# Seven block products in every feed-forward stage, with the modulation products moved to TensorE

## The chip, the cores and the metric

The kernel runs on one core of a Trainium2 chip. The metric is the device time of one execution in microseconds (us), from the first to the last instruction with what lies around them. All inputs are float32.

## The reference

Two layers over 640 tokens of width 1024: 512 latent tokens and 128 context tokens. Each layer has a feed-forward network (FFN), a token mixer (attention in layer 0, a gated recurrence in layer 1) and a second FFN. Each of these three is normalised before and after, shifted, scaled and gated by vectors that come from a modulation map.

```python
FFN_HIDDEN = ((8 * D_MODEL // 3 + 127) // 128) * 128          # 2816
def ada_pre(x, mod, j, g):
    return rmsnorm(x, g) * (1 + scale) + shift
def ada_post(x, y, mod, j, g, res_w):
    return x + res_w * gate * rmsnorm(y, g)
def swiglu(h, w_in, w_out):
    a, b = jnp.split(h @ w_in, 2, axis=-1)
    return (jax.nn.silu(a) * b) @ w_out
mod_ctx_all = jnp.einsum('d,lde->le', jax.nn.silu(c_ctx), w_mod) + b_mod
mod_lat_all = jnp.einsum('bd,lde->lbe', jax.nn.silu(c), w_mod) + b_mod[:, None]
```

The modulation map `w_mod` is 2 x 1024 x 9216: 36 column blocks of 512 over both layers, each multiplied by two vectors (latent and context).

## The kernel before

Activations lie transposed, features on partitions and the 640 tokens along the free axis, in two groups of 320 (`NG`). Each matrix is kept as a high part and a low part, so one product of a 128 x 128 weight tile with 320 tokens is three matmuls: high by high, high by low, low by high (in `run_jobs`, L444 and L449).

There are six stages in a row: p0 (FFN of layer 0), p1 (attention), p2 (second FFN of layer 0), p3 (FFN of layer 1), p4 (recurrence), p5 (second FFN of layer 1). A stage is a list of jobs. A plain job is one weight unit of up to eight 128 x 128 tiles against one or both groups. An FFN stage has 22 pairs of input-projection units (a gate unit and a value unit, 8 tiles each) whose results become one row block of `G`, and, after each part of the pairs, eight output-projection units that add that part's share into `Y`. Before the change `THIRDS` cuts the pairs into 7, 7 and 8. The first four pairs form the head: group 0 of all four, then group 1, so that the previous stage's normalisation of group 1 (`chain_gen`, with `post_gen` and `pre_gen`) can run meanwhile. The last eight output units form the tail: group 0 first, then group 1; five of these units lie in `H`, which is free by then.

In p5 alone, pairs from `FAST_FIRST` = 7 on are done in another way (`seven`): the pair is taken as a 2 x 2 block matrix (gate and value by the two halves of the 1024 features) and the activations as 2 x 2 blocks (feature halves by token groups), and the product is made of seven block products instead of eight, Winograd's form of Strassen's scheme. A block product (`product`, L476) is 4 tiles x 3 = 12 matmuls, so a pair takes 84 matmuls where the plain way takes 96. It needs sums of activation blocks, made once per stage by `sums_gen` into `T23` (in the place of `X`, which is spilled to DRAM by `spill_x` and read back by `unspill_x`), `T4` and the second half of `H`, and sums of weight blocks, made per pair on VectorE in `Quarter.follow`.

Weights come from DRAM by one queue (SyncE) into four raw buffers (`wraw`), are split by ScalarE (high part, L358) and VectorE (low part, L360) into a ring `whl` of eight quarters, of which a whole unit takes two and a quarter unit one. `prepare` converts ahead as far as `reach` and the ring allow.

Modulation blocks that are not needed at the start are made in the background of p0, p2 and p3 (12, 12 and 8 blocks, `mod_gen`): two loads of 1 MB bring a block of 1024 x 512, VectorE multiplies its eight 128-row tiles by the two vectors and adds them up (L763, L765: 16 instructions of 128 x 512 a block), and four matmuls of 32 x 256 with a matrix of ones sum over partitions (L775). `step_bg` takes one step of the first background generator at fixed places in the jobs. A first part of the modulation, before p0, is made by matmuls on 32 columns of the array (L871).

The order on each engine is that of the built program: a recording layer may move an instruction ahead of others that its inputs don't wait for, so engine order isn't source order.

## Time and profile before

| | |
|---|---|
| median of 3 runs | 2843.31 us (2841.24 to 2843.76) |
| profiled execution | 2848.25 us, its span 2846.3 us |
| TensorE matmul (PE) busy | 2775.4 us, 98% |
| VectorE (DVE) busy | 1849.1 us, 65% |
| ScalarE (ACT) busy | 1062.7 us, 37% |
| DMA share, mean rate | 33%, 100 GB/s |

The span is from the first to the last instruction of the profiled execution; 1.95 us lie around it. Busy times are unions over the whole span, so they say nothing of a single stage: the rows below are cut by stage. PE counts each fp32 matmul of the modulation as two instructions, and each 128 x 320 matmul as one.

### The profile page before, as it was taken

Reading aid. Unit: us, or ns where it says so; the run is one execution under the profiler, and the core shown is the slowest. Engines: PE = TensorE matmul, PEld = TensorE weight load, DVE = VectorE, ACT = ScalarE, POOL = GpSimd, SP = SyncE. Lnnn points to the kernel's source line nnn. Section 1 sums busy time; section 2 is a strip of 40 time slices with the busy share of each in tenths; the row PEclk is TensorE's granted clock in tenths of the full one; section 3 lists DMA queues with packets and bytes.
Section 4 is the critical chain, followed back from the end, with each engine's and each line's share of the span. In section 5 each row is a group of like instructions: output and inputs, shape, how many; then the busy total and the mean of one; then the engine's idle time right before and its main releaser. Section 6 shows DMA issues by size and latency. Waiting matters only on the chain.

```text
span 2846.3 us, 46837 instructions
## 1 busy us (share of the span) xinstructions
PE 2775.4 (98%) x19098; PEld 2710.3 (95%) x19098; DVE 1849.1 (65%) x3845; ACT 1062.7 (37%) x2100; POOL 0.2 (0%) x4
## 2 busy tenths in 40 slices
PE   7999999899998999999999999999999999999998
PEld 5999999899998999999999999999999999999997
DVE  6756653887777756656763554387667678656674
ACT  4222123466674422223332212243333345344453
POOL 0000000000000000000000000000000000000000
PEclk8999999999998999999999999999999999999999
DMA  8644433121123344445233433321121123323241
GB/s 265 185 134 148 147 111 90 43 59 52 46 72 97 109 136 138 153 140 163 60 100 108 130 123 89 89 61 49 56 60 56 56 59 104 87 70 92 73 133 38
DMA packets 424691, 283.32 MB, mean 100 GB/s; under 512 B 8442, under 2 KB 385820, under 8 KB 424220
## 3 DMA queue, kind: packets, MB, share of 16 engines
q1 hardware_dynamic: 423968, 280.13, 32.8%
q8 instruction: 150, 2.46, 0.4%
q14 instruction: 65, 0.53, 0.1%
q10 hardware_dynamic: 508, 0.20, 0.0%
HBM read 272.96 MB, written 7.34 MB: 98 GB/s over the span
## 4 chain that ended last, share of the span: by engine, by line
PE 89%; DVE 5%; ACT 4%; DMA 1%; issue 1%; ACTq 0%; DVEq 0%
PE mmps L444 48%; PE mmps L449 24%; PE mmps L476 6%; PE aux L1567 2%; PE mmps L1406 1%; PE aux L1375 1%; DMA wraw<-in_ffn_w_out 1%; DVE whl L360 1%; PE aux L514 1%; ACT p L1305 1%; PE aux L775 1%; PE aux L526 1%; PE aux L1376 1%; PE aux L1604 1%; ACT sq L1638 0%
## 5 line engine op out<-in xcount | busy, mean ns | idle before, releaser
L444 PE MATMUL mmps<-H,whl 128*128 128x320 f32 x6272 | 1256.3, 313 | 8.4 <-ACT H L603 6.6
L444 PEld LDWEIGHTS mmps<-H,whl 128*128 128x128 f32 x6272 | 1003.9, 189 | 22.6 <-issue 9.1
L449 PE MATMUL mmps<-H,whl 128*128 128x320 f32 x3136 | 786.0, 312 | 0.7 <-DVE whl L360 0.7
L358 ACT ACTIVATE whl<-wraw 128x1024 fp32r<-128x1024 f32 (+2 forms) x384 | 361.4, 941 | 1104.4 <-issue 533.1
L360 DVE TENSOR_TENSOR whl<-wraw,whl 128x1024 fp32r<-128x1024 f32 (+2 forms) x384 | 413.4, 1077 | 348.2 <-ACT whl L358 343.9
L449 PEld LDWEIGHTS mmps<-H,whl 128*128 128x128 f32 x3136 | 544.2, 189 | 1.1 <-DVE whl L360 1.0
L444 PE MATMUL mmps<-G,whl 128*128 128x320 f32 x2368 | 471.2, 312 | 6.1 <-ACT G L971 1.7
L444 PEld LDWEIGHTS mmps<-G,whl 128*128 128x128 f32 x2368 | 378.7, 189 | 12.6 <-issue 3.3
L765 DVE SCALAR_TENSOR_TENSOR macc<-wmod,CV,macc 128x512 f32<-128x512 f32 x448 | 306.7, 748 | 0.0
L449 PE MATMUL mmps<-G,whl 128*128 128x320 f32 x1184 | 295.2, 311 | 0.0
L444 PE MATMUL mmps<-G,H 128*128 128x320 f32 x960 | 217.2, 313 | 0.1
L449 PEld LDWEIGHTS mmps<-G,whl 128*128 128x128 f32 x1184 | 204.9, 189 | 0.0
L444 PEld LDWEIGHTS mmps<-G,H 128*128 128x128 f32 x960 | 161.7, 189 | 0.4 <-ACT Y L1133 0.4
L1135 DVE TENSOR_TENSOR Y<-Y,mmps 128x320 f32<-128x320 f32 x144 | 67.2, 485 | 140.8 <-PE mmps L449 140.1
L449 PE MATMUL mmps<-G,H 128*128 128x320 f32 x480 | 149.9, 312 | 0.0
L969 DVE TENSOR_TENSOR gm<-sa,mmps 128x320 f32<-128x320 f32 x146 | 65.9, 484 | 123.3 <-PE mmps L449 122.6
L476 PE MATMUL mmps<-H,whl 128*128 128x320 f32 x720 | 113.0, 310 | 1.0 <-ACT gm L994 1.0
L476 PEld LDWEIGHTS mmps<-H,whl 128*128 128x128 f32 x720 | 107.4, 188 | 1.2 <-ACT gm L994 1.2
L444 PE MATMUL mmps<-H,G 128*128 128x320 f32 x448 | 104.6, 315 | 0.0
L548 DVE TENSOR_TENSOR acc<-acc,sq 128x320 f32<-128x320 f32 x168 | 80.6, 489 | 24.9 <-ACT sq L547 23.8
L449 PEld LDWEIGHTS mmps<-G,H 128*128 128x128 f32 x480 | 90.8, 189 | 0.0
L476 PE MATMUL mmps<-T,whl 128*128 128x320 f32 x540 | 86.6, 310 | 0.0
(259 smaller groups left out, 2923.7 us busy)
## 6 DMA issues: line engine op xcount, KB each, us to landing
wraw<-in_ffn_w_in SPq DMA_DIRECT2D x192, 512.0 KB, 4.0
wmod<-in_w_mod SPq DMA_DIRECT2D x66, 1024.0 KB, 6.1
wraw<-in_ffn_w_out SPq DMA_DIRECT2D x64, 448.0 KB, 3.8
wraw<-in_hgrn_w_in SPq DMA_DIRECT2D x40, 512.0 KB, 3.9
wraw<-in_ffn_w_out SPq DMA_DIRECT2D x32, 512.0 KB, 4.2
wraw<-in_attn_w_in SPq DMA_DIRECT2D x24, 512.0 KB, 3.9
wm<-in_w_mod SPq DMA_DIRECT2D x4, 1024.0 KB, 11.0
wraw<-in_attn_w_out SPq DMA_DIRECT2D x8, 512.0 KB, 4.0
```

The costliest lines, as they stand in the source:

```text
L358: nc.scalar.activation(out=u.w[0][:, 0:nk, :], in_=src, func=AF.Copy)
L360: self.los.append(lambda: nc.vector.tensor_tensor(out=u.w[1][:, 0:nk, :], in0=src, in1=u.w[0][:, 0:nk, :].bitcast(F32), op=ALU.subtract))
L444: nc.tensor.matmul(out=ps[g][:, 0:NG], lhsT=w[0][:, a, :], rhs=rhs[:, r, b, g * NG:(g + 1) * NG], start=(i == 0 and r == 0), stop=False,)
L449: nc.tensor.matmul(out=ps[g][:, 0:NG], lhsT=w[1][:, a, :], rhs=rhs[:, 0, b, g * NG:(g + 1) * NG], start=False, stop=(i == last),)
L476: nc.tensor.matmul(out=ps[:, 0:NG], lhsT=w[a][:, k, :], rhs=j.operand(r, k), start=(j.first and k == 0 and n == 0), stop=(k == 3 and n == ...
L514: self.nc.tensor.matmul(out=ps[:, c0 + n:c0 + n + 1], lhsT=acc[:, b0:b0 + 128], rhs=self.ones, start=True, stop=True,)
L526: self.nc.tensor.matmul(out=ps[:, c0 + b0 + p0:c0 + b0 + 128], lhsT=y[:, n:n + 1].to_broadcast([128, 128]), rhs=self.ident[:, p0:128], sta ...
L548: return lambda: nc.vector.tensor_tensor(out=acc, in0=acc, in1=sq, op=ALU.add)
L765: nc.vector.scalar_tensor_tensor(out=acc[s], in0=w, scalar=cv, in1=acc[s], op0=ALU.mult, op1=ALU.add)
L969: nc.vector.tensor_tensor(out=t, in0=st[g], in1=ps, op=ALU.mult)
L1135: nc.vector.tensor_tensor(out=y, in0=y, in1=ps, op=ALU.add)
L1567: nc.tensor.matmul(out=ps[:, c * 128:(c + 1) * 128], lhsT=km[:, c * 128:(c + 1) * 128], rhs=self.view(Q2, c * 128, dims), start=True, stop ...
```

## The change

All four FFN stages take pairs 4 to 21 by seven block products (`FAST`); only the four head pairs stay plain. The parts become 4, 5, 6 and 7 pairs, so each stage has four rounds of output units instead of three, with the same matmuls in total. X is spilled and the activation sums are made in each stage, right behind the head. Half of `T4` moves into row block 7 of `G`, which no part uses any more. The modulation blocks are multiplied on TensorE (`mod_rows`): eight matmuls of 32 x 512 a block, four at a time on different 32 columns, straight from the loaded weights; the matrix of ones goes. Away from products only three raw buffers are filled ahead and at most three whole units stand in the ring.

```diff
-THIRDS = (range(0, 7), range(7, 14), range(14, 22))
+PARTS = (range(0, 4), range(4, 9), range(9, 15), range(15, 22))
-GAP0 = 2
-GAP2 = 2
-GAP3 = 3
+GAP0 = 1
+GAP2 = 1
+GAP3 = 2
-FAST_FIRST = 7
+FAST = range(4, 22)
+PLAIN_RAWS = 3
...
     def place(self, u):
+        if u.quarters == 2 and sum(x.quarters == 2 for x in self.ring) >= HL_BUFS:
+            return False
...
-        if self.first[n] == self.n_conv - 1:
+        near = self.jobs[n:n + 6]
+        if not any(isinstance(j, Product) for j in near):
             self.flush_lo()
+            self.ensure_dma(self.raw_done + PLAIN_RAWS - 1)
+        elif self.first[n] == self.n_conv - 1:
+            self.flush_lo()
...
+    def mod_rows(self, ps, CS, ts, i, half, first, last):
+        for k in range(4 * half, 4 * half + 4):
+            g = k % 4
+            self.nc.tensor.matmul(
+                out=ps[g * 32:(g + 1) * 32, 0:512], lhsT=CS[:, k, 30 - 2 * i:62 - 2 * i], rhs=ts[half][:, g, :],
+                start=first and half == 0, stop=last and half == 1, skip_group_check=True,
+            )
...
         for i in range(n):
-            acc = [self.mod_p.tile([128, 512], F32, name="macc", tag=f"macc{s}") for s in range(2)]
-            for k in range(KT):
-                w = ts[k // 4][:, k % 4, :]
-                for s in range(2):
-                    for _ in range(gap):
-                        yield
...
-                if k % 4 == 3 and i + 1 < n:
-                    ts[k // 4] = self.mod_load(first + i + 1, k // 4)
-            yield
+            for _ in range(16 * gap):
+                yield
             ps = self.aux_tile()
...
+            for half in range(2):
+                self.mod_rows(ps, CS, ts, i, half, True, True)
+            if i + 1 < n:
+                ts = [self.mod_load(first + i + 1, h) for h in range(2)]
+            yield
...
-        self.T4 = self.fast.tile([128, 2, 4, NG], F32R, name="T4")
+        low = self.G[:, :, 7, :].rearrange("p r (k t) -> p r k t", k=2)
+        high = self.fast.tile([128, 2, 2, NG], F32R, name="T4")
+        self.T4 = [low[:, :, 0, :], low[:, :, 1, :], high[:, :, 0, :], high[:, :, 1, :]]
...
     def fast_hooks(self, jobs, last_plain):
+        last_plain.after.append(self.spill_x)
         last_plain.after.append(lambda: self.bg.insert(0, gen))
...
-        for part, third in enumerate(THIRDS):
+        for part, third in enumerate(PARTS):
             for jj, j in enumerate(third):
-                if fast and j >= FAST_FIRST:
+                if j in FAST:
                     jobs += seven(jj, j)
                     continue
...
-        if fast:
-            head[-1].after.append(self.spill_x)
+        self.fast_hooks(jobs, head[-1])
...
+        if mods:
+            jobs[-16].before.append(lambda: self.drain([self.modgen]))
```

On TensorE in p2, around one modulation block. A row is a line, an instruction, what it writes and reads, and how many follow each other. Before, among output jobs (`G` by `whl`):

```order
L449 MATMUL mmps<-G,whl 128x320 x2
L444 MATMUL mmps<-G,whl 128x320 x4
L449 MATMUL mmps<-G,whl 128x320 x2
L775 MATMUL aux<-macc,one 32x256 x4
L444 MATMUL mmps<-G,whl 128x320 x4
L449 MATMUL mmps<-G,whl 128x320 x2
```

And of the change, from one block to the next, in the stretch of block products of the second part (`T_10060` is `T23`, `T_10061` the new half of `T4`, and `G` its other half):

```order
L763 MATMUL aux<-wmod,CS 32x512 x8
L484 MATMUL mmps<-T_10060,whl 128x320 x12
L484 MATMUL mmps<-H,whl 128x320 x12
L484 MATMUL mmps<-T_10060,whl 128x320 x12
L484 MATMUL mmps<-H,whl 128x320 x12
L484 MATMUL mmps<-G,whl 128x320 x6
L484 MATMUL mmps<-T_10061,whl 128x320 x6
L484 MATMUL mmps<-H,whl 128x320 x24
L484 MATMUL mmps<-T_10060,whl 128x320 x12
L484 MATMUL mmps<-H,whl 128x320 x12
L763 MATMUL aux<-wmod,CS 32x512 x8
```

TensorE now reads the loaded block (`wmod`) itself, and 108 matmuls stand between two blocks. In the built program this distance is 108, with a few of 102 or 114, for 17 of the 32 blocks, 204 or more for the blocks of p3, and 60 and 63 once each in p0 and p2, between the second and the third block and the first and the second.

On SyncE's queue at the beginning of p2, where loads of weights (`wraw`) and of modulation blocks (`wmod`) are issued in order. Before:

```order
L708 DMA wmod<-in_w_mod 128x4x512
L322 DMA wraw<-in_ffn_w_in 128x8x128 x8
L708 DMA wmod<-in_w_mod 128x4x512
L322 DMA wraw<-in_ffn_w_in 128x8x128 x2
L708 DMA wmod<-in_w_mod 128x4x512
L322 DMA wraw<-in_ffn_w_out 128x7x128 x6
L708 DMA wmod<-in_w_mod 128x4x512
```

And of the change:

```order
L716 DMA wmod<-in_w_mod 128x4x512 x2
L322 DMA wraw<-in_ffn_w_in 128x8x128 x7
L888 DMA xs<-X 128x5120
L322 DMA wraw<-in_ffn_w_out 128x4x128 x4
L716 DMA wmod<-in_w_mod 128x4x512 x2
L322 DMA wraw<-in_ffn_w_out 128x4x128 x3
L716 DMA wmod<-in_w_mod 128x4x512 x2
L322 DMA wraw<-in_ffn_w_out 128x4x128
```

Both halves of a block are now issued together, behind the matmuls of the block before, which release the buffers; the spill of X stands between the head's loads, and four output units' loads stand ahead of the second block's.

On VectorE in p2, at the output units of the first part. Before, products and sums of the modulation (`macc`) between the low parts of weights:

```order
L360 TENSOR_TENSOR whl<-wraw,whl 128x896
L765 SCALAR_TENSOR_TENSOR macc<-wmod,CV,macc 128x512 x5
L360 TENSOR_TENSOR whl<-wraw,whl 128x896
L360 TENSOR_TENSOR whl<-wraw,whl 128x1024 x2
L763 TENSOR_SCALAR macc<-wmod,CV 128x512
L782 TENSOR_TENSOR ms<-ms,aux 128x256
```

And of the change, the end of the sums of activation blocks (L924 to L939, L916 the low parts of their splits):

```order
L916 TENSOR_TENSOR H<-nt,H 128x320
L362 TENSOR_TENSOR whl<-wraw,whl 128x512
L916 TENSOR_TENSOR T_10060<-nt,T_10060 128x320
L938 TENSOR_TENSOR nt<-H,nt 128x320
L916 TENSOR_TENSOR T_10060<-nt,T_10060 128x320
L362 TENSOR_TENSOR whl<-wraw,whl 128x512
L135 TENSOR_TENSOR s_10310<-wraw 128x512
L939 TENSOR_TENSOR nt<-nt,H 128x320
L137 TENSOR_TENSOR wraw<-wraw 128x512
L916 TENSOR_TENSOR T_10061<-nt,T_10061 128x320
L362 TENSOR_TENSOR whl<-wraw,whl 128x512 x4
```

The `macc` instructions are gone, and the sums end just ahead of the weight sums and splits of the first pairs that are done by block products.

## Rows read from the trace of the kernel before

**Rows 1.** The page: the span and the engines' busy times.
```profile
span 2846.3 us, 46837 instructions
PE 2775.4 (98%) x19098; PEld 2710.3 (95%) x19098; DVE 1849.1 (65%) x3845; ACT 1062.7 (37%) x2100; POOL 0.2 (0%) x4
```

**Rows 2.** Windows of p0 to p3 and p5: PE, PEld, DVE, ACT, POOL; clock, DMA.
```profile
36.20:529.50 493.30, 488.96 (x3336) 475.24 (x3337) 304.16 (x533) 139.92 (x235) 0.00 (x0) 0.99 0.45 135
529.50:917.80 388.30, 363.98 (x2481) 345.56 (x2479) 307.25 (x837) 239.66 (x578) 0.00 (x0) 0.97 0.22 64
917.80:1401.40 483.60, 482.98 (x3314) 474.73 (x3315) 308.58 (x558) 136.09 (x234) 0.00 (x0) 0.99 0.42 127
1401.40:1882.60 481.20, 478.65 (x3290) 472.28 (x3289) 259.62 (x487) 136.55 (x236) 0.00 (x0) 1.00 0.34 102
...
2373.50:2846.30 472.80, 456.73 (x3103) 452.19 (x3102) 295.60 (x585) 205.49 (x416) 0.00 (x0) 0.98 0.29 86
```

**Rows 3.** Windows in p5: plain output jobs, then 7.5 pairs by block products.
```profile
2616.00:2666.00 50.00, 50.00 (x342) 49.94 (x341) 22.26 (x38) 10.30 (x15) 0.00 (x0) 1.00 0.25 73
2666.00:2758.00 92.00, 92.00 (x630) 92.00 (x629) 71.78 (x128) 53.40 (x109) 0.00 (x0) 1.00 0.31 88
```

**Rows 4.** Timeline of TensorE around one modulation block in p2.
```profile
1064.36 0.46 PE L449 MATMUL mmps<-G,whl 128*128 128x320 f32 x2
1064.74 0.64 PE L775 MATMUL aux<-macc,one 128*32 128x256 f32 x8
1065.31 0.85 PE L444 MATMUL mmps<-G,whl 128*128 128x320 f32 x4
```

**Rows 5.** Timeline of TensorE, modulation matmuls of the start.
```profile
44.26 1.06 PE L871 MATMUL mmps<-wmod,CS 128*32 128x512 f32 x8
45.14 1.90 PE L871 MATMUL mmps<-Y,CS 128*32 128x512 f32 x16
```

**Rows 6.** Groups by line: the modulation on VectorE and TensorE; busy us, mean ns.
```profile
L765 DVE SCALAR_TENSOR_TENSOR macc<-wmod,CV,macc 128x512 f32<-128x512 f32 x448 | 306.7, 748 | 0.0
L763 DVE TENSOR_SCALAR macc<-wmod,CV 128x512 f32<-128x512 f32 x64 | 30.1, 483 | 61.1 <-PE aux L775 61.0
L775 PE MATMUL aux<-macc,one 128*32 128x256 f32 x256 | 20.5, 391 | 0.0
```

**Rows 7.** DMA issues: count, size of one, median us to landing.
```profile
wraw<-in_ffn_w_in SPq DMA_DIRECT2D x192, 512.0 KB, 4.0
wmod<-in_w_mod SPq DMA_DIRECT2D x66, 1024.0 KB, 6.1
wm<-in_w_mod SPq DMA_DIRECT2D x4, 1024.0 KB, 11.0
xs<-X SPq DMA_DIRECT2D x1, 2560.0 KB, 8.4
```

**Rows 8.** Timeline of VectorE in p5: part of the activation sums.
```profile
2475.88 0.49 DVE L925 TENSOR_TENSOR nt<-H 128x320 f32<-128x320 f32 x1
2476.28 0.49 DVE L930 TENSOR_TENSOR nt<-H 128x320 f32<-128x320 f32 x1
```

**Rows 9.** Timeline of TensorE in p0's head, around a wait.
```profile
60.58 0.46 PE L444 MATMUL mmps<-H,whl 128*128 128x320 f32 x2
63.12 0.51 PE L449 MATMUL mmps<-H,G 128*128 128x320 f32 x1 [2.08 <-DVE G L360]
63.42 0.73 PE L444 MATMUL mmps<-H,G 128*128 128x320 f32 x2
...
66.62 0.50 PE L444 MATMUL mmps<-H,G 128*128 128x320 f32 x2
66.96 0.31 PE L449 MATMUL mmps<-H,G 128*128 128x320 f32 x1
```

**Rows 10.** Waits among p5's block products, 2666 to 2758: total us, times, longest.
```profile
ACT whl L358 <- PE mmps L476: 28.0, 38, 1.3
DVE s L134 <- DMA wraw<-in_ffn_w_in: 5.8, 6, 1.3
```

More of the change, by code (lines that the diff above doesn't have):

```diff
@@ L274, in setup @@
         self.CV = c.tile([128, KT, 2], F32, name="CV")
-        self.one = c.tile([128, 64], F32, name="one")
         self.ones = c.tile([128, 1], F32, name="ones")
@@ L382, in prepare @@
                 self.raw_done += 1
-        if self.first[n] == self.n_conv - 1:
+        near = self.jobs[n:n + 6]
[3 more added lines that the diff above has]
+        elif self.first[n] == self.n_conv - 1:
             self.flush_lo()
     def more_dma(self):
-        self.flush_lo()
-        self.ensure_dma(self.raw_done + RAW_BUFS - 1)
+        near = self.jobs[self.cur:self.cur + 6]
+        if any(isinstance(j, Product) for j in near):
+            self.flush_lo()
+            self.ensure_dma(self.raw_done + RAW_BUFS - 1)
     def held(self, kt):
@@ L754, in mod_gen @@
         for i in range(n):
[L755 to L778 removed]
+            for _ in range(16 * gap):
+                yield
+            ps = self.aux_tile()
+            for half in range(2):
+                self.mod_rows(ps, CS, ts, i, half, True, True)
+            if i + 1 < n:
+                ts = [self.mod_load(first + i + 1, h) for h in range(2)]
+            yield
             if i == 0:
[L780 removed]
+                nc.scalar.activation(out=ms, in_=ps[:, 0:512], func=AF.Copy)
             else:
[L782 removed]
+                nc.vector.tensor_tensor(out=ms, in0=ms, in1=ps[:, 0:512], op=ALU.add)
             yield
         yield
[L785 removed]
+        self.mod_fin([(first, n)], ms, self.aux_tile(), False)
         for p in range(first // 2, (first + n) // 2):
@@ L797, in startup @@
         S = self.st_p
-        CS = S.tile([128, KT, 34], F32, name="CS")
+        CS = self.mod_p.tile([128, KT, 62], F32, name="CS", tag="CS")
         nc.sync.dma_start(out=self.ident, in_=A["k_ident"])
@@ L841, in startup @@
         )
-        nc.vector.tensor_copy(CS[:, :, 2:4], self.CV)
+        self.mod_vectors(CS)
         ps = self.aux_tile()
@@ L867, in startup @@
             for i in range(2):
-                ts = loads[2 * half + i]
-                for k in range(KT):
-                    g = k % 4
-                    nc.tensor.matmul(
-                        out=ps[g * 32:(g + 1) * 32, :], lhsT=CS[:, k, 2 - 2 * i:34 - 2 * i],
-                        rhs=ts[k // 4][:, k % 4, :], start=(i == 0 and k < 4), stop=(i == 1 and k >= 4),
-                        skip_group_check=True,
-                    )
+                for h in range(2):
+                    self.mod_rows(ps, CS, loads[2 * half + i], i, h, i == 0, i == 1)
             nc.scalar.activation(out=ms, in_=ps[:, 0:512], func=AF.Copy)
@@ L941, in sums_gen @@
             yield from put(b, self.T23[:, 0, 0, k, :], self.T23[:, 0, 1, k, :])
-            yield from put(d, self.T4[:, 0, k, :], self.T4[:, 1, k, :])
+            yield from put(d, self.T4[k][:, 0, :], self.T4[k][:, 1, :])
             yield
@@ L953, in fast_hooks, with ffn_jobs @@
         products[-1].after.append(self.unspill_x)
-    def ffn_jobs(self, l, s, mods, gap, close, fast=False):
+    def ffn_jobs(self, l, s, mods, gap, close):
         nc = self.nc
@@ L977, in y_done @@
         def y_done(f, part):
-            return lambda ps, g: self.y_part(f, ps, g, part == 0, part == 2)
+            return lambda ps, g: self.y_part(f, ps, g, part == 0, part == len(PARTS) - 1)
         def seven(jj, j):
```

38 lines of the change are left out of this document (9 added, 29 removed).

## The prediction

> **What bounds the kernel now.** I read the page first, then windows cut at the stages, then the timeline of TensorE inside them. On the page TensorE's matmuls are busy for 2775.4 of 2846.3 us and VectorE for 1849.1 [rows 1]. The cut by stages says the same of each FFN stage: in p0, p2 and p3 TensorE is busy for 488.96 of 493.30, 482.98 of 483.60 and 478.65 of 481.20 us, in p5 for 456.73 of 472.80, while VectorE is busy for 304.16, 308.58, 259.62 and 295.60 us of them [rows 2]. So within a stage TensorE's instruction stream is the path, and a matmul less is time less, as long as nobody makes TensorE wait.
>
> What one matmul is worth comes from stretches in which it never waits: 342 in 50.00 us of plain output jobs and 630 in 92.00 us of block products, both 146 ns each [rows 3]. A block product's matmul costs no more than a plain one, and its VectorE work (71.78 of 92.00 us) fits under it.
>
> **The change, part by part. The products.** In p0, p2 and p3 18 pairs a stage go from 96 to 84 matmuls, 3 x 18 x 12 = 648; in p5, where 15 were done so already, 3 more pairs, 36. Together 684 x 0.146 us = 99.9 us less. The cuts into four parts add none: the output units have the same tiles in total.
>
> **The modulation on TensorE.** 32 blocks. What goes: one block's eight instructions on ones begin at 1064.74, and the two 128 x 320 matmuls ahead of them began at 1064.36; the next follow at 1065.31 [rows 4]. The two take 0.29 us, to 1064.65, so a block held TensorE for 0.66 us, and 32 for 21.1. That is a little more than its busy time of 20.5 us [rows 6]. What comes: eight matmuls of 32 x 512 a block, 16 instructions in the trace. At the start 8 of them begin at 44.26 and the next 16 at 45.14, 0.88 us later [rows 5]; 16 therefore take 1.76 us. Rows 4 show what surrounds them in a stretch of 128-wide matmuls: 0.66 us where two rounds over 256 columns take half of 0.88, 0.44; so 0.22 us is spent on changing over. A block then costs 1.76 + 0.22 = 1.98 us, 32 cost 63.4, and the net addition is 63.4 - 21.1 = 42.3 us.
>
> The rows say that four such instructions run at once on different 32 columns: eight of L775's, each lasting 391 ns [rows 6], fit into the 0.66 us. The Trainium skill (TensorE: Matmul & The Clock Gate, Part 3: Packing small matmuls) gives less for packing, 3.07x measured for four row tiles and 2.38x for three column tiles. By that page's 3.07 in place of 4 a block would cost an estimated 1.76 x 4 / 3.07 + 0.22 = 2.51 us and the sum would be 17 us worse; the trace has the same instruction in the same form, so I go by the trace.
>
> VectorE loses 306.7 + 30.1 us of products [rows 6]. It isn't the path, so this gives nothing directly; it pays for the work of the block products.
>
> So far -99.9 + 42.3 = -57.6 us.
>
> **Waits for the modulation's loads.** Before, VectorE waited for a block; now TensorE, in order, and everything of TensorE is queued behind. A block's two loads of 1 MB go out only when the block before has released the buffers, and the weight loads behind them in SyncE's queue wait with them. One alone lands in 6.1 us, four at once in 11.0 [rows 7]. For 17 blocks 108 matmuls stand between, 108 x 0.146 = 15.8 us: more than either, so 0; the bound above is 2 us each, if weight loads are in the way in SyncE's queue. Twice only 60 or 63 matmuls stand there, 8.8 and 9.2 us; and in p2 the queue holds four output units' loads ahead, the last of which waits for a raw buffer, so for a conversion. Between nothing (6.1 us and a little) and 8 us (11.0 and a blocked queue of some 6 us) I take 3 us each, nearer to the row for four at once. A wait is followed by slow matmuls: after 2.08 us of waiting in p0, the 13 matmuls from 63.12 to 66.62 begin 0.27 us apart, the 1.2 GHz level [rows 9]; at 0.146 they would take 1.9 us instead of 3.5, so 1.6 us are lost. Twice 4.6 us makes +9.
>
> **The activation sums.** They stand in every stage now, between the head and the third product of pair 4, behind 192 output matmuls and 24 of two products: 216 x 0.146 = 31.5 us. VectorE has 56 instructions a stage, which begin 0.40 us apart [rows 8], 22.4 us. In the same time it splits eight output units of 512 columns and the first quarters, at 71.78 us for 7.5 pairs [rows 3], 9.6 a pair: some 14 us. That is 36 against 31.5, but sums whose inputs are ready stand ahead of the head's end. Late by 0 to 5 us a stage; I take 0.5, +2 in all. Spilling X lands in 8.4 us [rows 7] and begins during the head's first half, when X is final: hidden.
>
> **The rest.** Without `macc`, the head of p0 may lose its wait of 2.08 us and the slow stretch behind it [rows 9]: between 0 and -3.7, I take -2. Three whole units in the ring and three raw buffers ahead: a head job lasts 24 x 0.146 = 3.5 us and a load lands in 4.0 [rows 7], so three loads in flight cover it; in the attention and recurrence stages the bodies' order on TensorE stays as it was. I take 0, between -3 and +6. In block products four raw buffers stay; the loads share the channel with the modulation, but ScalarE waits there mostly for ring places that TensorE frees (28.0 us against 5.8 us of waiting for loads on VectorE [rows 10]), so weights are split well ahead: 0, above 4.
>
> **The sum.** -57.6 + 9 + 2 - 2 = -48.6 us. The sum was made against the profiled execution, 2848.25 us, of which 1.95 lie outside its span; that one ran 4.94 us above the median of the runs shown. The change takes the same number from either: 2843.3 - 48.6 = 2794.7 us, 2795 rounded.
>
> **Rivals.** *Waits of some size everywhere.* If the sums come late by 4 us in each of four stages and the 17 close blocks wait 1 us each, 33 us come on top of the sum: 2828, at about 2806 to 2837 in all. For it: VectorE's 36 us against 31.5. Against it: in p5 the block products themselves never made TensorE wait for VectorE.
>
> *Nothing waits.* If the loads arrive and p0's head wait goes with its slow stretch, the sum is -57.6 - 3.7: 2782, reaching down to 2775 with something gained in the plain stages. For it: 6.1 us a load against 8.8.
>
> *Slower, through the clock.* TensorE now stops for DMA. If each of the 29 waited-for blocks (32 less the first of each stage) cost 2.0 us or more in all, the 57.6 us would be gone; with a wait of 2 us and the slow stretch of 1.6 behind it that is 29 x 3.6 = 104 us, 2890 us in all. It takes loads that are late by 2 us at 15.8 us distance, that is 17.8 us for what the slowest row has at 11.0. The Trainium skill (TensorE: Matmul & The Clock Gate, section HAM oscillation) has it as a rule that a matmul kernel which waits for DMA in each tile falls back to the slow clock each time. By that rule the trace agrees on a single wait, in rows 9, and shows none that repeats.
>
> *It doesn't do what it says.* If VectorE or ScalarE bounded the products, 12 matmuls less would give nothing; VectorE at 71.78 / 92.00 = 78% and ScalarE at 53.40 / 92.00 = 58% in them [rows 3] speak against it; a 512-wide addition a block, at most the 748 ns of L765 [rows 6] in 17.8 us, makes it 82%. It lies within the last two cases below.
>
> **How the numbers follow.** Forecast (2782 to 2806): 0.63. Nothing waits, or better (below 2782): 0.13. Waits everywhere (2806 to 2837): 0.18. No change within 0.2% (5.7 us, about what a measurement can tell): 0.03. Slower: 0.03. The predicted time is 2795; the range from 2777 to 2817 leaves out a little below and half of the second rival above. Faster has 0.63 + 0.13 + 0.18 = 0.94.
>
> **What would show it.** Right: p0, p2 and p3 last about 460 to 470 us, p5 about 467; no group of block products waits; modulation blocks take 2 us each with TensorE waiting for `wmod` only at one block each in p0 and p2. Wrong: waits on `wmod` at many blocks and a granted clock below 1 in those stages; TensorE waiting for the sums' low parts at the third product of a stage; or an attention stage longer than its 388.3 us [rows 2].

## The result, and the profile after

The median of four runs is 2781.02 us (2780.47 to 2782.12), against 2843.53 (2841.24 to 2845.24) for the kernel before in the same session: ratio 0.9781, interval 0.9764 to 0.9798. The predicted time was 2795, the range 2777 to 2817. The time is inside the range, 14 us below the forecast, where I had put the rival that nothing waits.

The page of the kernel after, against [rows 1]:

```profile
span 2778.7 us, 47467 instructions
...
PE 2715.6 (98%) x18670; PEld 2613.1 (94%) x18670; DVE 1977.8 (71%) x4285; ACT 1307.3 (47%) x2693; POOL 0.2 (0%) x4
```

The profiled execution took 2780.47 us, its span 67.6 us less than before's. The medians differ by 62.5 us: the profiled run of the kernel before ran 4.7 us above its median, so some 5 us of what follows are the spread of these two runs. The windows of p0 to p5, cut at the same matmuls as in [rows 2] (columns: stretch, its length, busy time of PE, PEld, DVE, ACT, POOL, clock, DMA share, GB/s):

```profile
36.70:513.90 477.20, 471.48 (x3223) 445.06 (x3223) 326.98 (x642) 216.36 (x420) 0.00 (x0) 0.99 0.48 151
513.90:891.90 378.00, 362.38 (x2466) 344.39 (x2467) 298.10 (x814) 240.29 (x579) 0.00 (x0) 0.97 0.19 56
891.90:1360.90 469.00, 466.86 (x3202) 444.29 (x3200) 329.77 (x669) 215.28 (x421) 0.00 (x0) 1.00 0.46 144
1360.90:1825.30 464.40, 461.84 (x3143) 445.15 (x3143) 329.09 (x669) 213.06 (x420) 0.00 (x0) 1.00 0.40 123
1825.30:2313.60 488.30, 480.25 (x3467) 473.43 (x3468) 355.01 (x789) 192.57 (x384) 0.00 (x0) 1.00 0.20 58
2313.60:2778.70 465.10, 450.71 (x3068) 446.65 (x3066) 320.01 (x645) 218.39 (x451) 0.00 (x0) 0.99 0.29 88
```

p0, p2 and p3 are 16.1, 14.6 and 16.8 us shorter, p5 is 7.7 shorter. Of the lengths that the prediction gave as signs of being right, 460 to 470 us, p0 with 477.2 misses; its own terms give 493.3 - 31.5 + 12 x 1.32 = 477.6 for p0, so that sign was set wrong, not the sum. The line that I had not expected is the second: p1, the attention, whose body the change doesn't touch, is 10.3 us shorter than its 388.3. TensorE stays busy in nearly all of each FFN stage, and VectorE has more to do in p0 (326.98 us for 304.16) although the modulation's sums have left it.

Two windows in p5 answer to [rows 3]:

```profile
2558.00:2608.00 50.00, 50.00 (x342) 49.88 (x341) 25.82 (x44) 16.18 (x29) 0.00 (x0) 1.00 0.30 90
2608.00:2700.00 92.00, 92.00 (x629) 91.90 (x628) 67.19 (x120) 50.11 (x100) 0.00 (x0) 1.00 0.29 83
```

342 and 629 matmuls, as before 342 and 630: the price of one has not moved. The timeline of TensorE around a modulation block among block products of p0 answers to [rows 4, 5] (columns: start, length of the row, instruction):

```profile
137.56 1.92 PE L484 MATMUL mmps<-H,whl 128*128 128x320 f32 x12
139.41 1.92 PE L763 MATMUL aux<-wmod,CS 128*32 128x512 f32 x16
141.26 2.02 PE L484 MATMUL mmps<-H,whl 128*128 128x320 f32 x12
143.12 1.92 PE L484 MATMUL mmps<-T,whl 128*128 128x320 f32 x12
144.88 1.92 PE L484 MATMUL mmps<-H,whl 128*128 128x320 f32 x12
```

Twelve matmuls undisturbed take 1.76 us, from 143.12 to 144.88. From 137.56 to 143.12 stand 24 of them and one block: 5.56 - 2 x 1.76 = 2.04 us for a block. The groups of TensorE and the DMA issues answer to [rows 6, 7]:

```profile
L763 PE MATMUL aux<-wmod,CS 128*32 128x512 f32 x512 | 64.7, 599 | 0.0
```

```profile
wmod<-in_w_mod SPq DMA_DIRECT2D x66, 1024.0 KB, 7.1
...
xs<-X SPq DMA_DIRECT2D x4, 2560.0 KB, 12.8
```

TensorE was idle for 0.0 us ahead of its 512 modulation instructions: no wait for `wmod` at all. A load of a modulation block now lands in 7.1 us where it took 6.1, the spill of X in 12.8 for 8.4. The view of the tile `wmod` gives the ends too, and SyncE's queue shows the place in p2 with 63 matmuls between two blocks:

```profile
DMA to landing us min/median/max: 5.0/7.1/9.6
```

```profile
942.03 1.23 SPq L716 DMA_DIRECT2D wmod<-in_w_mod  x2
```

The second of these loads goes out at 942.9 and lands 7.0 us later, at 949.9; its block begins at 952.2, 2.3 us after that.

The end of the sums on VectorE in p5 and the first block products on TensorE, against [rows 8]:

```profile
2392.08 0.88 DVE L916 TENSOR_TENSOR T<-nt,T 128x320 fp32r<-128x320 f32 x2
```

```profile
2405.90 3.68 PE L484 MATMUL mmps<-H,whl 128*128 128x320 f32 x24
2409.42 1.92 PE L484 MATMUL mmps<-T,whl 128*128 128x320 f32 x12
```

The last two low parts end at 2392.96, 12.9 us ahead of the first product, and the third product, the first that needs a sum, begins 24 matmuls later without a pause. In p0's head the wait of [rows 9] has shrunk to 0.23 us, and the matmuls behind it begin 0.147 us apart:

```profile
62.80 0.42 PE L457 MATMUL mmps<-H,G 128*128 128x320 f32 x1 [0.23 <-DVE G L362]
63.05 0.46 PE L452 MATMUL mmps<-H,G 128*128 128x320 f32 x2
63.35 0.31 PE L457 MATMUL mmps<-H,G 128*128 128x320 f32 x1
```

The longest sum of waits among p5's block products, 2600 to 2692, is of the kind of [rows 10]: ScalarE waits 22.4 us in all for places in the ring.

**Where p1's 10.3 us came from.** p1's window ends at the first matmul of p2's head. Ahead of it, at the joint, group 0 of p1 is normalised while TensorE runs p1's output products of group 1. The inverse root of the norm is a chain of thirteen instructions of 0.16 us on VectorE, from `rs_v` to the third `rs_y`. In the kernel before, VectorE's timeline there reads (left out between these rows are further links of the chain and other work):

```profile
906.89 0.16 DVE L521 TENSOR_SCALAR rs_v<-aux 128x3 f32<-128x3 f32 x1 [0.99 <-PE aux L514]
906.96 0.74 DVE L765 SCALAR_TENSOR_TENSOR macc<-wmod,CV,macc 128x512 f32<-128x512 f32 x1
...
908.24 0.74 DVE L765 SCALAR_TENSOR_TENSOR macc<-wmod,CV,macc 128x512 f32<-128x512 f32 x1
...
911.25 1.22 DVE L360 TENSOR_TENSOR G<-wraw,G 128x1024 fp32r<-128x1024 f32 x1
...
914.77 0.15 DVE L509 SCALAR_TENSOR_TENSOR rs_y<-rs_a,rs_y 128x3 f32<-128x3 f32 x1
```

From 906.89 to 914.77 are 7.9 us: VectorE put two products of the modulation, two low parts of weights and additions to `acc` between the links, and stood idle for 1.22 us of them itself. TensorE ran out of output products, as the kernel before's waits of TensorE from 903 to 920 show (the first is for L514, which sums `acc` over the partitions, so for the additions as well as for the chain):

```profile
PE aux L514 <- DVE rs_y L509: 3.8, 1, 3.8
```

Waits of 0.6 us for `rs_y` and 1.2 for `H` follow it.

In the kernel after, the same chain is through in 3.5 us, with one low part of a weight in it, and the view of TensorE's waits has no row there:

```profile
881.27 0.16 DVE L529 TENSOR_SCALAR rs_v<-aux 128x3 f32<-128x3 f32 x1 [0.63 <-PE aux L522]
881.35 1.21 DVE L362 TENSOR_TENSOR whl<-wraw,whl 128x1024 fp32r<-128x1024 f32 x1
...
884.78 0.16 DVE L517 SCALAR_TENSOR_TENSOR rs_y<-rs_a,rs_y 128x3 f32<-128x3 f32 x1
```

This could come from the modulation's products having left VectorE, or from the new order of weights.

The other end of p1's window has changed too, at the joint of p0 with p1. The kernel before waits 22.6 us behind p1's first matmul, inside p1's window (529.5 to 917.8):

```profile
552.18 1.44 PE L514 MATMUL aux<-ones,acc 128*128 128x1 f32 x6 [3.33 <-DVE acc L548]
```

The kernel after doesn't have this wait; it waits at the end of p0's window instead:

```profile
511.14 0.80 PE L522 MATMUL aux<-ones,acc 128*128 128x1 f32 x6 [2.35 <-DVE rs_y L517]
...
513.90 1.17 PE L452 MATMUL mmps<-H,whl 128*128 128x320 f32 x3 [1.23 <-ACT H L611]
```

So part of p1's gain was only moved, into p0. The experiments had to tell these apart, and to say why the loads that I had feared were never waited for.

### The profile page after: what moved, and what is told of

It reads as the page before. It is cut to its first block, busy times and chain, and to the rows that moved or that the text cites. A ratio compares the mean times of both kernels' runs of the same rounds, so it can differ in the third digit from the quotient of the medians.

```text
span 2778.7 us, 47467 instructions
## 1 busy us (share of the span) xinstructions
PE 2715.6 (98%) x18670; PEld 2613.1 (94%) x18670; DVE 1977.8 (71%) x4285; ACT 1307.3 (47%) x2693; POOL 0.2 (0%) x4
## 4 chain that ended last, share of the span: by engine, by line
PE 89%; DVE 5%; ACT 4%; DMA 1%; issue 1%; ACTq 0%; DVEq 0%; SPq 0%
PE mmps L484 31%; PE mmps L452 30%; PE mmps L457 15%; PE aux L1564 2%; PE aux L763 2%; PE mmps L1403 1%; DVE whl L362 1%; PE aux L1372 1%; ACT p L1302 1%; PE aux L1373 1%; PE aux L522 1%; PE aux L1601 1%; PE aux L534 1%; ACT whl L360 1%; ACT sq L1635 0%
## 5 line engine op out<-in xcount | busy, mean ns | idle before, releaser
L360 ACT ACTIVATE whl<-wraw 128x512 fp32r<-128x512 f32 (+4 forms) x644 | 464.2, 722 | 661.3 <-PE mmps L452 369.6
L362 DVE TENSOR_TENSOR whl<-wraw,whl 128x512 fp32r<-128x512 f32 (+4 forms) x644 | 515.3, 801 | 207.8 <-ACT whl L360 199.6
L452 PE MATMUL mmps<-H,whl 128*128 128x320 f32 x2624 | 571.5, 317 | 9.3 <-ACT H L611 6.9
L484 PE MATMUL mmps<-H,whl 128*128 128x320 f32 x3456 | 544.1, 309 | 0.1
L484 PEld LDWEIGHTS mmps<-H,whl 128*128 128x128 f32 x3456 | 515.3, 188 | 10.5 <-issue 4.2
L452 PE MATMUL mmps<-G,whl 128*128 128x320 f32 x2448 | 487.7, 311 | 3.8 <-ACT G L1649 1.5
L452 PEld LDWEIGHTS mmps<-H,whl 128*128 128x128 f32 x2624 | 432.5, 191 | 19.5 <-ACT H L611 8.3
L457 PE MATMUL mmps<-H,whl 128*128 128x320 f32 x1312 | 369.6, 314 | 0.7 <-DVE whl L362 0.7
L484 PE MATMUL mmps<-T,whl 128*128 128x320 f32 x2160 | 352.5, 309 | 0.0
L484 PEld LDWEIGHTS mmps<-T,whl 128*128 128x128 f32 x2160 | 325.4, 188 | 5.0 <-issue 2.5
L457 PEld LDWEIGHTS mmps<-H,whl 128*128 128x128 f32 x1312 | 239.1, 191 | 1.1 <-DVE whl L362 1.0
L452 PE MATMUL mmps<-G,H 128*128 128x320 f32 x880 | 198.7, 312 | 0.1
L452 PEld LDWEIGHTS mmps<-G,H 128*128 128x128 f32 x880 | 147.8, 189 | 0.3 <-ACT Y L1130 0.3
L457 PE MATMUL mmps<-G,H 128*128 128x320 f32 x440 | 137.3, 312 | 0.0
L997 ACT ACTIVATE sa<-sa 128x320 f32<-128x320 f32 x144 | 67.9, 471 | 66.4 <-DVE sa L1000 65.5
L135 DVE TENSOR_TENSOR s<-wraw 128x512 f32<-128x512 f32 x72 | 49.7, 690 | 69.0 <-DMA wraw<-in_ffn_w_in 68.9
## 6 DMA issues: line engine op xcount, KB each, us to landing
xs<-X SPq DMA_DIRECT2D x4, 2560.0 KB, 12.8
```

Of the source, the lines that this page charges most:

```text
L135: V.tensor_tensor(out=z, in0=a[:, lo], in1=b[:, lo], op=ALU.subtract)
L360: nc.scalar.activation(out=u.w[0][:, 0:nk, :], in_=src, func=AF.Copy)
L362: self.los.append(lambda: nc.vector.tensor_tensor(out=u.w[1][:, 0:nk, :], in0=src, in1=u.w[0][:, 0:nk, :].bitcast(F32), op=ALU.subtract))
L452: nc.tensor.matmul(out=ps[g][:, 0:NG], lhsT=w[0][:, a, :], rhs=rhs[:, r, b, g * NG:(g + 1) * NG], start=(i == 0 and r == 0), stop=False,)
L457: nc.tensor.matmul(out=ps[g][:, 0:NG], lhsT=w[1][:, a, :], rhs=rhs[:, 0, b, g * NG:(g + 1) * NG], start=False, stop=(i == last),)
L484: nc.tensor.matmul(out=ps[:, 0:NG], lhsT=w[a][:, k, :], rhs=j.operand(r, k), start=(j.first and k == 0 and n == 0), stop=(k == 3 and n == ...
```

## The experiments

Each ratio is against runs of the kernel before on the same chip in the same session (medians 2843.05 to 2845.5); by it the changed kernel stands at 0.9781.

**The modulation alone moved, on the kernel before.** The whole of `mod_gen` and the gaps as in the change, nothing else.

```diff
-GAP0 = 2
+GAP0 = 1
...
+            for half in range(2):
+                self.mod_rows(ps, CS, ts, i, half, True, True)
+            if i + 1 < n:
+                ts = [self.mod_load(first + i + 1, h) for h in range(2)]
```

> The kernel before with the modulation products alone on TensorE. Theory M (the multiply-adds of the modulation on VectorE stood inside the normalisation chain and made TensorE wait where p0 hands over to p1 and p1 to p2): 2843.5 + 44 - 12 = 2876, with the waits of 3.6 us at p0's end and of 4 us at p1's end gone. Rival R (these waits went with the ring, the buffers or the products, not with the modulation): 2888, and both waits as before. A price of the blocks as I predicted it alone (1.98 - 0.66 each, 42 us) would give 2886 under R and 2874 under M, too near to tell from theirs.

Measured: 2877.1 us, ratio 1.0114 (1.0099 to 1.0129): theory M's 2876, and slower than before. The windows say where:

```profile
35.90:541.80 505.90, 502.96 (x3433) 476.30 (x3434) 189.09 (x341) 139.88 (x235) 0.00 (x0) 1.00 0.43 132
541.80:922.10 380.30, 361.33 (x2475) 343.02 (x2474) 299.45 (x816) 239.79 (x578) 0.00 (x0) 0.98 0.20 57
```

p0 is 12.6 us longer than in [rows 2], for twelve blocks, and p1 8.0 us shorter; the chain at its end takes 3.5 us (rows `rs_v` at 911.43 to `rs_y` at 914.95), and TensorE has no wait there. The other half of theory M is wrong: at the joint of p0 with p1 the wait of 3.33 us for `acc` is still there, at 564.44. The modulation isn't its cause.

**The modulation alone moved back, on the kernel after.**

```diff
...
-            for half in range(2):
-                self.mod_rows(ps, CS, ts, i, half, True, True)
...
+            for k in range(KT):
...
+                    if k == 0:
+                        nc.vector.tensor_scalar(out=acc[s], in0=w, scalar1=cv, scalar2=None, op0=ALU.mult)
+                    else:
+                        nc.vector.scalar_tensor_tensor(
+                            out=acc[s], in0=w, scalar=cv, in1=acc[s], op0=ALU.mult, op1=ALU.add
+                        )
```

> The changed kernel with its modulation products back on VectorE. Theory (the move to TensorE is paid with 2.04 us a block and buys VectorE's time): the 32 blocks give TensorE back 44 us, but VectorE then has 327 + 12 x 16 x 0.74 = 469 us of work in p0, where TensorE has 477 - 12 x 1.4 = 460, and about as much in p2, so it is the bound there; p0 465 to 480, p2 460 to 475, p3 (8 blocks, 329 + 95 us) about 455, the joint before p2 some 10 us longer again, together 2765 to 2795. Rival (VectorE keeps up, only TensorE's own instructions count): 2781 - 44 + 12 = 2749, or 2737 if the joint keeps its gain.

Measured: 2767.39 us, ratio 0.9730 (0.9714 to 0.9746): 14 us faster than the changed kernel. The windows of p0 to p3:

```profile
33.40:502.40 469.00, 461.06 (x3126) 442.49 (x3126) 430.54 (x832) 213.92 (x418) 0.00 (x0) 0.99 0.51 156
502.40:886.10 383.70, 362.60 (x2473) 344.23 (x2473) 305.77 (x835) 239.31 (x578) 0.00 (x0) 0.98 0.22 63
886.10:1354.40 468.30, 459.83 (x3104) 447.06 (x3104) 435.55 (x864) 213.46 (x421) 0.00 (x0) 0.98 0.47 144
1354.40:1807.30 452.90, 450.13 (x3073) 443.28 (x3073) 385.52 (x768) 214.38 (x421) 0.00 (x0) 0.99 0.40 120
```

p1 is 5.7 us longer again, with TensorE's waits of 3.8, 1.2 and 0.6 us as in the kernel before, to the tenth. With the run above this settles the joint of p1 with p2: both directions move it, by 5.7 and 8.0 us. It isn't all of p1's 10.3: with the modulation on VectorE in both, p1 takes 383.7 us for 388.3. These 4.6 us belong to the joint of p0 with p1: this run has the kernel after's waits there (2.35 and 1.24 us ahead of p1's first matmul) and not the wait of 3.33 us. The run with the ring of before, next, has them too, so it is the block products and the new parts that moved this wait.

The theory's time and its lengths of the stages held, but for the joint, put at 10 us: p0 gains 8.2 us where 12 blocks at 1.4 us were to be had, p2 next to nothing, p3 11.5. Its reason in p0 is not shown: VectorE is busy for 430.54 of 469.00 us there, near its limit but not at it as my sum of 469 us had it.

Read together, the four kernels price each half of the change. The block products, with the parts and the ring, gain 77 us when VectorE has the modulation (1 - 0.9730) and 95 us when TensorE has it (1.0114 - 0.9781). The move of the modulation costs 32 us on the kernel before and 14 us beside the block products. What the prediction called paying for the work of the block products is there, 18 us of it; it is less than the price.

**The ring and the raw buffers as before, on the kernel after.**

```diff
-        if u.quarters == 2 and sum(x.quarters == 2 for x in self.ring) >= HL_BUFS:
-            return False
...
-        self.ensure_dma(PLAIN_RAWS - 1)
+        self.ensure_dma(RAW_BUFS - 1)
```

> The changed kernel with the ring of weights and the count of raw buffers as in the kernel before (no limit of three whole units, four raw buffers, low parts flushed as before). Theory (this part of the change is worth nothing): 2778 to 2787, stage times within 2 us of the changed kernel's. Rival (it carries the gain at the joints): 2791 to 2795, with p1 near 388 again.

Measured: 2782.66 us (2780.99 to 2784.69), ratio 0.9782 (0.9768 to 0.9797), p1 377.8. This part of the change is worth nothing, as the prediction took it.

**Modulation blocks closer together: half, and a quarter of the steps.**

```diff
-            for _ in range(16 * gap):
+            for _ in range(8 * gap):
```

> The changed kernel with half of the steps between one modulation block and the next, some 60 matmuls (8.8 us, 10.8 with the block) in p0 and p2: the distance at which I predicted a wait of 3 us for the loads of wmod. Theory (loads issued right behind a block land in 5.0 to 7.1 us as a rule, so 8.8 us hide them, and only a load of 9.6 us is late): 2780 to 2785, at most three waits of under 1.5 us. Rival (my prediction): a wait of 3 us with 1.6 us of slow clock at most of 24 blocks, 2830 to 2890; half as large at half of them 2795 to 2810.

Measured: 2785.57 us (2778.87 to 2788.7), ratio 0.9790 (0.9775 to 0.9805), which the spread doesn't tell from the changed kernel, and no matmul that waits for `wmod`. Of the 24 blocks of p0 and p2, 12 stand 60 or 66 matmuls behind the one before, the distance for which I had charged 9 us. Seven stand closer still, some 36 to 44 matmuls, because the built program takes their two halves apart:

```profile
88.81 1.06 PE L763 MATMUL aux<-wmod,CS 128*32 128x512 f32 x8
...
91.17 1.06 PE L763 MATMUL aux<-wmod,CS 128*32 128x512 f32 x8
```

```diff
-            for _ in range(16 * gap):
+            for _ in range(4 * gap):
```

> The changed kernel with the modulation blocks closer: a quarter of the steps between one block and the next, some 36 matmuls (5.3 us, 7.3 with the block) in p0 and p2, 60 (8.8 us) in p3. Theory (the waits that I predicted didn't come because the blocks were 17.9 us apart and a load lands in 7.1 us, at most 9.6): now the loads are late in p0 and p2, 24 blocks by 0.3 to 2.5 us, 2788 to 2840, with waits of the block's first matmul for wmod in the trace. Rival (the two buffers and the order of the queues always hide the load): 2779 to 2784, no such wait. Rival through the clock: waits of over 3 us at 24 places and a granted clock below 0.97, over 2840.

Measured: 2796.27 us, ratio 0.9830 (0.9815 to 0.9845), 15 us above the changed kernel. TensorE's waits; the longest of them, with what follows on TensorE; and a window around it:

```profile
PE aux L763 <- DMA wmod<-in_w_mod: 7.0, 5, 2.5
```

```profile
119.05 1.06 PE L763 MATMUL aux<-wmod,CS 128*32 128x512 f32 x8 [2.52 <-DMA wmod<-in_w_mod]
...
120.44 0.45 PE L452 MATMUL mmps<-G,whl 128*128 128x320 f32 x2
120.73 0.31 PE L457 MATMUL mmps<-G,whl 128*128 128x320 f32 x1
```

```profile
115.00:120.00 5.00, 2.48 (x19) 1.41 (x17) 2.64 (x7) 1.41 (x3) 0.00 (x0) 1.00 0.65 230
```

Only 5 blocks are waited for, 7.0 us in all; a load lands in 5.5 us (median), at most 10.3. p0 grows by 11.1 us and p2 by 7.0, so another 11 us have to come from elsewhere. Not from the clock: it is 1.00 around these waits, and behind the longest two matmuls take 0.29 us, the undisturbed pace. But 18 of the 24 blocks are taken apart here, their halves mostly 15 or 16 matmuls from each other, and each half pays for changing to 32 columns and back: the half at 122.58 holds TensorE from 122.48 to 123.67, 1.19 us, so a block costs 2.38 for 2.04, and 18 blocks 6 us more (an estimate from these numbers). Another 1.5 us are waits for ScalarE's high parts; the rest is open. The wait sets in at about these distances: five of the blocks here are late, and of the seven at 36 to 44 matmuls in the run above none.

**No output products between the head and the block products.**

```diff
-PARTS = (range(0, 4), range(4, 9), range(9, 15), range(15, 22))
+PARTS = (range(0, 6), range(6, 11), range(11, 16), range(16, 22))
...
-        last_plain.after.append(self.spill_x)
...
+        head[2 * HEAD].after.append(self.spill_x)
```

> The changed kernel with parts of 6, 5, 5, 6 pairs, so that the block products of pairs 4 and 5 follow the four plain pairs directly and no output products lie between (as many matmuls as before in all). The sums of activations take VectorE 19.3 us of its own time in each stage, and 37 to 52 us from their first instruction to their last beside the other work; the first two products need none of them and take some 7 us. Theory (the 28 us of output products of the first part cover the sums, which is why my term of 2 us for late sums came out as nothing): each of the four stages now waits 10 to 25 us, 2821 to 2881. Rival (the sums would be in time anyway): 2779 to 2790.

Measured: 2816.86 us, ratio 0.9899 (0.9885 to 0.9914): 36 us above the changed kernel, just under the theory's range. In the profiled execution p0, p2, p3 and p5 are 5.1, 8.6, 9.0 and 10.6 us longer. A window at the first block products of p5:

```profile
2400.00:2420.00 20.00, 14.76 (x75) 13.15 (x74) 17.24 (x40) 8.20 (x19) 0.00 (x0) 0.83 0.07 20
```

75 matmuls where the 20 us before, at a clock of 1.00, held 138: 63 x 0.146 = 9 us lost here. TensorE's timeline names what it waited for:

```profile
2404.60 0.41 PE L484 MATMUL mmps<-H,whl 128*128 128x320 f32 x1 [0.76 <-DVE H L916]
...
2405.81 0.56 PE L484 MATMUL mmps<-T,whl 128*128 128x320 f32 x2 [0.50 <-DVE T L916]
2408.72 0.41 PE L484 MATMUL mmps<-H,whl 128*128 128x320 f32 x1 [2.36 <-ACT H L914]
2410.23 0.64 PE L484 MATMUL mmps<-H,whl 128*128 128x320 f32 x1 [1.09 <-DVE H L916]
```

L914 and L916 are the splits of the sums. In p5 the 28 us of output products are what hides them. In the other stages this is only in part so: there TensorE waits for the sums 0.57 us in p2, 1.42 in p3 and not at all in p0. What p0, p2 and p3 lose is to a good part at their ends, where TensorE waits longer than in the kernel after:

```profile
PE aux L522 <- DVE rs_a L515: 8.3, 3, 3.1
```

The order has a second effect that I had not thought of. The last part has six pairs, so the tail's group 1, beside which group 0 is normalised, has 144 matmuls, where the changed kernel has 168 and the kernel before 192. At the end of p0, up to p1's first matmul, TensorE waits 4.4 us here and 3.6 in the changed kernel, and not at all in the kernel before. That these waits follow the length of the tail fits all three kernels; no run changes the tail alone.

**Three plain pairs.** This order changes the activations that come out, for a reason that stays open, so only its time is read.

```diff
...
-HEAD = 4
+HEAD = 3
...
-FAST = range(4, 22)
+FAST = range(3, 22)
```

> The changed kernel with 19 of 22 pairs by block products and three plain pairs ahead of them, parts of 3, 5, 7, 7 pairs. Theory (matmuls alone count as long as the sums are covered): 48 matmuls fewer in all, 7.0 us, and the sums, which end 12 to 15 us before the first product now, still end 5 to 8 us before it: 2772 to 2777. Rival (with a shorter start the weights of the first products or the sums come late): a wait of 3 to 10 us in each stage, 2786 to 2814.

Measured: 2794.48 us, ratio 0.9829 (0.9812 to 0.9845): the rival's time. The products' own waits are small (block products wait for no load), but TensorE's waits at the joints grow: for `rs_y` 6.7 us at 5 places (4.2 at 4 in the kernel after), for `acc` 5.0 at 4 (3.9 at 2), for `H` 8.0 at 9 (6.9 at 6). A shorter head leaving less to hide the normalisation behind fits this; it is read from one profile and not tested apart.

**The modulation on both engines.** Since the version with VectorE was faster than the change, I looked for a mix. First, 15 blocks on VectorE in halves of 256 columns:

```diff
...
+            if i in vec:
+                yield from self.mod_vec(i, ts, ms)
...
+        acc = self.mod_p.tile([128, 2, 256], F32, name="macc", tag="macc")
```

> The changed kernel with 15 of its 32 modulation blocks on VectorE, in halves of 256 columns: four of twelve in p0 and in p2, every second one from the second to the eighth, and seven of eight in p3; the others stay on TensorE. Theory (VectorE has room in p3, where it was busy 329 of 464 us, and some in p0 and p2 away from the joints, so each block moved gives TensorE 2.04 us less about 0.95 for the sums over rows): 15 x 1.1 = 16 us, 2762 to 2769, with the joint before p2 as short as in the changed kernel. Rival (VectorE near its limit makes TensorE wait wherever multiply-adds are put in): 2775 to 2790.

Measured: 2778.08 us, ratio 0.9767 (0.9752 to 0.9781), the rival's time. On VectorE its 420 multiply-adds take 183.2 us: half the columns take 477 ns where the whole take 748, so a block costs VectorE 13.5 us ((183.2 + 19.4) / 15, with 19.4 us for the first product of each half) where whole columns cost 10.5 ((306.7 + 30.1) / 32 [rows 6]); VectorE was busy for 404 of 461.5 us in p3, and of 16 us 3 were left. Whether VectorE's load is the reason, as the rival has it, is open: in p0, where nothing was gained, it was busy for 370 of 478 us. Then whole columns, p0 and p3 on VectorE and p2 on TensorE, two steps from one product to the next:

```diff
+VEC_GAP = 2
+MOD_PLAN = {4: (("v", 4, 12),), 16: (("t", 16, 12),), 28: (("v", 28, 8),)}
...
+        for kind, a, m in MOD_PLAN[first]:
+            yield from (self.mod_vec(a, m, delay) if kind == "v" else self.mod_ten(a, m, gap, delay))
...
```

> The changed kernel with the modulation products of p0 and p3 on VectorE at full width (512 columns, 0.74 us each, as in the kernel before) and those of p2 on TensorE. Theory (a block costs TensorE 2.04 us by its own matmuls and 0.7 to 0.9 us by VectorE, and VectorE's multiply-adds hurt only at the joint of p1 with p2 and where VectorE is full, as the version with all of them on VectorE showed by p0 469.1, p1 383.7, p2 468.4, p3 452.9): p0 469, p1 378, p2 469, p3 453, together 2759 to 2764. Rival (what p0 and p3 gained there is lost again when p2 keeps TensorE): 2767 to 2781.

Measured: 2769.36 us, ratio 0.9739 (0.9726 to 0.9753), the rival's range again, but not for its reason: p0 468.3, p1 377.5 and p2 469.2 came as the theory had them, and p3 is 461.7 for 453. And with p0 and p2 split in time (against this version):

```diff
-MOD_PLAN = {4: (("v", 4, 12),), 16: (("t", 16, 12),), 28: (("v", 28, 8),)}
+MOD_PLAN = {4: (("t", 4, 4), ("v", 8, 8)), 16: (("t", 16, 6), ("v", 22, 6)), 28: (("v", 28, 8),)}
```

> As the version with p0 and p3 on VectorE, but each of p0 and p2 split in time: the first four blocks of p0 and the first six of p2 on TensorE, the later eight and six on VectorE. Theory (VectorE is fullest in the first eighty us of each stage and has room in its middle, where it was busy 18 to 29 of 39 us): p0 467 to 471, p2 460 to 464, p3 453, together 2751 to 2758. Rival (at 16 multiply-adds in some 34 steps VectorE is full wherever they stand, and p2 gains nothing): 2759 to 2766.

Measured: 2767.9 us, ratio 0.9734 (0.9721 to 0.9747), above both ranges: p0 471.7, p2 465.6, p3 460.9. p2 gains 3.4 us where 8 were expected, p3 is off as before. Last, p0 all on VectorE, p2 split, and p3's products three steps apart as they were in the first version with VectorE:

```diff
-VEC_GAP = 2
-MOD_PLAN = {4: (("t", 4, 4), ("v", 8, 8)), 16: (("t", 16, 6), ("v", 22, 6)), 28: (("v", 28, 8),)}
+VEC_GAP = {4: 2, 22: 2, 28: 3}
+MOD_PLAN = {4: (("v", 4, 12),), 16: (("t", 16, 6), ("v", 22, 6)), 28: (("v", 28, 8),)}
...
```

> The split plan with p0 wholly on VectorE as in the version that gave 468.3 there, p2 with six blocks on TensorE and six on VectorE as in the split plan (465.6), and p3 on VectorE with its multiply-adds wider apart (three steps from one to the next for two). Theory (what VectorE's multiply-adds cost beside TensorE's work depends on how densely they stand: p3 took 452.9 us where they were three steps apart and 460.8 to 461.7 where they were two): p3 453 again, p0 468 to 469, p2 465 to 466, together 2754 to 2759. Rival (the density is not it, and p3's 8 us went with the ring of weights or the order of the stage): p3 460 to 462, 2763 to 2768.

Measured: 2760.96 us (2759.41 to 2763.78), ratio 0.9712 (0.9699 to 0.9726), between the two ranges and the fastest of all, 20 us below the changed kernel. Its windows of p2 and p3:

```profile
879.70:1345.10 465.40, 461.73 (x3162) 443.99 (x3160) 389.86 (x780) 215.83 (x422) 0.00 (x0) 1.00 0.48 150
1345.10:1802.10 457.00, 451.41 (x3078) 444.27 (x3078) 389.38 (x781) 213.94 (x420) 0.00 (x0) 0.99 0.40 121
```

p3 came to 457.0, between the theory's 453 and the rival's 460. The distance of the products would be worth 3.9 us of the 8, from one profile each; p4, whose work none of these runs changes, spreads over 4.4 us. The rest was my reading: the 453 stood for less than p3. In the version with all on VectorE p3's first 40 us have no wait of TensorE, while its joint wait (4.2 us, `L523` for `rs_a`) stands ahead of the cut, in p2's window; here p3's first 40 us hold waits of 2.03, 0.50 and 0.54 us. Over p2 and p3 together that version took 921.2 us, this one 922.4, the split plan 926.5, the changed kernel 933.4.

## Why the prediction was right, and where it was off

**TensorE is the path.** Right: the page has it at 98%, and the price of a matmul is as it was. The pairs of runs give 95 us for the predicted 99.9 where TensorE has the modulation, and 77 where VectorE has it.

**The price of a block.** 1.98 us predicted, 2.04 measured, so the net addition is 32 x (2.04 - 0.66) = 44.2 for 42.3. By the packing figure of the Trainium skill (TensorE: Matmul & The Clock Gate, Part 3: Packing small matmuls), which it has for four row tiles, I had estimated 2.51 us. For these matmuls, four at a time on different 32 columns, the rows give the lower 2.04.

**Waits for the loads, +9: the step that failed.** It was that two loads issued together behind a block, with weights in the queue, take between 6.1 and 11.0 us and more, and that 8.8 us of distance fall short by 3. Measured, they land in 7.1 us, at most 9.6, at the close place in p2 2.3 us ahead of their block, and the run with half of the steps has twelve blocks at that distance and no wait. I had priced two loads by a row for four at the start. The fear of SyncE's queue had no row behind it, and at that place the two loads go out at 942.03, not behind weights.

**The sums, +2.** 0 here: they end 12.9 us ahead. The sum of 36 against 31.5 us had VectorE start them behind the head, though the prediction allowed for some ahead of its end; they begin during it, at 2355 in p5, 50 us before the first product. How much the output units in front matter differs by stage: without them TensorE waits for the sums 4.7 us in p5 and loses 9, in p2 and p3 it waits 0.6 and 1.4, in p0 not at all.

**p0's head, -2.** The wait of 2.08 us is gone and with it the slow stretch, 3.7 us. p0's length doesn't show them, because the new waits of 2.35 and 1.23 us stand at its end. In the versions where p0's modulation begins on VectorE it is back, 2.1 us for `G`; in the split plan, whose first four blocks of p0 are on TensorE, it is not.

**Ring and raws, 0.** Right, within 2 us.

**The parts, 0.** Right for the matmuls. But the last part is a pair shorter, and with it the tail beside which group 0 is normalised. Waits of 3.6, 2.0 and 3.0 us now stand at the ends of p0, p2 and p3, which no term had; the heads behind them have lost 3.3, 1.7 and 1.5 us of waits, so that on balance they cost little and mostly change the windows.

**What was missing.** I wrote that taking the products off VectorE "gives nothing directly", since VectorE isn't the path. At the joint of p1 with p2 it is: 5.7 to 8.0 of the 10.3 us in p1. I looked at busy shares by stage, where p1's 363.98 of 388.3 stood in [rows 2] with 24 us not busy, and did not ask what ended them.

**The account.** Products -100 and blocks +44 make -56; the span of the profiled executions fell by 67.6, the medians by 62.5. Of the other 11.5 in the profiles 10.3 are p1's and 2.5 each stand in p4 and p5, less some 4 in p3: 18 x 12 matmuls less 8 blocks' 11 us should have made it 20.7 us shorter, and it is 16.8. p3 begins behind a wait of 1.96 us for `H`, and its first 6 us run at a granted clock of 0.72; the rest of its 4 us stays open. p5 has lost three waits of the kernel before (0.98 us for `gm`, 0.17 and 0.75 for `G`). p4 stays open: its window took 487.7 to 492.1 us in the runs here, with the same work, so 2.5 us may be no more than that spread.

**The rivals.** *Nothing waits* is what happened as to the loads and the sums. That its 2782 is met to 1 us is luck in part: it knew neither of p1's 10.3 us nor of the 2.5 each in p4 and p5, and against them stand p3's 4, some 3 of the head's 3.7 in p0, 2 of the blocks' price and the 5 of the runs' spread. *Waits everywhere* shows a beginning in the run with a quarter of the steps, with five waits and 15 us. *Slower, through the clock* does not: around these five waits the granted clock is 1.00. "A wait is followed by slow matmuls" is not so at each wait: behind 2.08 us in [rows 9] they were slow, behind 2.52 us in that run they were not, and in the run without output products, with several waits close together, the clock was 0.83 over 20 us. What tells these apart no run here shows. That the change doesn't do what it says is refuted for the products; for the modulation the run that undoes it says that on this kernel the move costs 14 us more than it returns.

## What to carry to other kernels

An engine that is off the path by its busy share is on the path where a chain of short dependent instructions hands one stage to the next; look at what stands between the links before calling its work free, and move that work away from the joint before moving it to another engine. When a stage is cut into other parts, look at what the last part was hiding. Compare stages by their joints as well as by their windows: a wait that moves across a cut looks like a gain on one side. When work moves to the engine that bounds, price it against leaving most of it where it was at another place in time: here 12 blocks on VectorE in p0, 8 in p3 and half of p2's, kept away from one joint, beat all 32 on TensorE by 20 us. A load that hides is judged by landing times for as many transfers as are in flight there, not by the slowest row in the trace.

## What the runs showed of the hardware

On VectorE an instruction of 128 x 512 with a scalar takes 748 ns and one of 128 x 256 takes 477, so halving the columns saves 36%. Sixteen matmul instructions of 32 x 512, in fours on different columns, take 1.85 us, and the change to and from 128 columns 0.19. In the run without output products, in the stretch of 20 us that holds TensorE's four waits of 0.50 to 2.36 us for the sums, 4.7 us in all, the granted clock was 0.83, and 9 us of matmuls were lost, where TensorE was idle for 5.2. Behind a single wait of 2.52 us for a load, in the run with a quarter of the steps, it stayed at 1.00.
